# Layer-0 S5 scan: states stored with the blocks innermost and shifted by one chunk, block carries by doubling

## Chip, cores and metric

The kernel runs on one core of a Trainium2 chip. The metric is device time in microseconds (us) of one execution; a smaller number is better. Times of several executions are given as their median with the lowest and highest.

## What is computed

The reference is a stack of four decoder layers over a residual stream `x` of 256 tokens by 1024 channels (batch 1, fp32). Each layer normalises `x`, makes one wide input projection, runs a token mixer (layer 0: S5, 1: GLA, 2: differential attention, 3: Mamba-2 SSD), gates it, adds a cross attention to 256 memory tokens and projects back onto `x`. Only layer 0 matters here. Its mixer, cut to what matters:

```python
# u: 256 tokens x 2048 channels = 128 groups of 16; 64 complex states per group
dr, di = einsum('tgh,gph->tgp', u, bb_re), einsum('tgh,gph->tgp', u, bb_im)
s[t]   = lam_bar * s[t-1] + (dr, di)[t]          # complex, per group and state
y[t]   = einsum('gp,ghp->gh', s_re[t], c_re) - einsum('gp,ghp->gh', s_im[t], c_im) + d_skip * u[t]
g      = gelu(y);  out = g * sigmoid(g @ w_glu) * silu(z)
```

The recurrence is linear, so it can be cut: inside a chunk the response to the chunk's own tokens is a matrix product, and only the state at the chunk's border has to be carried.

## The kernel before, in words

**Tiling of the scan.** A chunk is 4 tokens, so there are 64 chunks. The 128 groups are worked in four units (`ub` 0 to 3) of 32 groups each, by `s5_unit` (line 598). Two groups with their 64 states fill the 128 partitions, so a unit has 16 columns of group pairs (four sub-blocks `sb` of four). A unit's states lie in a tile `E` of 128 partitions x 2 (real, imaginary) x 16 x 64 chunks.

**Steps of one unit.** For each `sb`, VectorE scales the B matrix by powers of lambda (`scaled`, L639 to L644, tiles `q` and `bu`), ScalarE copies it into a padded tile (L656), TensorE transposes it (L661), ScalarE evacuates that (`pm`, L662), TensorE multiplies it with the tokens `V` (L666) and ScalarE copies the chunks' own responses into `E` (L667, one copy of 512 columns). The same scaling gives the C matrix (`cu`, `cp`, L677) and the response inside a chunk (`kt`, L684, and `tm`, eight-buffer `cp`, two-buffer `tm`). Then VectorE runs the recurrence over the 64 chunks of `E`, taken as 8 blocks `J` of 8 chunks `i`:

- L706: seven local steps, each for all 8 blocks at once (`step`, L701 to L704: a product, one addition of the real factor's part, one subtraction, one addition);
- L708: seven carry steps over the blocks, each on the last chunk of one block (L698, L702 to L704 on 16 columns of groups);
- L712: the carry added to the first seven chunks of blocks 1 to 7 (L716 to L719), for the real and the imaginary part.

After a `yield` TensorE makes the output `y` (L730 from `tm` and `V`, L734 from `cp` and `E`, where chunk `j` reads state `j-1`, hence columns 1:64 from 0:63), and ScalarE applies gelu (L736).

In `E` the chunk number is 8J+i with `i` innermost, so one local step reads and writes every eighth float32 of a row, and the factor for a position (tile `lp`, L537) has the groups innermost.

**Order of the tokens.** `x` is loaded with its rows regrouped (L753) so that VectorE's 32x32 transposition (`evac_u`, L779) gives `V` by chunk. Layer 0 keeps this order through its projections; the tokens are put back in order where a result is split into a high and a low half for the output projection (`split`, L114 on ScalarE and L115 on VectorE, called from `xattn` at L428 and `evac_glu` at L847).

**What sets the order of the work.** `layer0` (L745) enlists projections as generators in `self.fill`: four steps of z, the u blocks 2 and 3, then q_mem and z_x (L225). It calls each unit up to its `yield` with raised priority, then gives out some fill (`tick`, 4, 4, 2, 2 steps), then the rest of the unit. A planner lays the instructions out in one fixed order per engine before the run, from those priorities and its own costs; on the chip each engine takes its list in order and waits on semaphores. `V` has two buffers, so the tokens of unit 2 are written after unit 0's output matmuls have read theirs. Powers and factors are made once in `s5_tables` (L500). Weights come by SP's DMA queue into five `raw` buffers.

Of the kernel before, what the change touches and what calls it, by code (L numbers as in the profile page):

```python
# [37 lines left out]
class Net:  # L38
# [139 lines left out]
    def trans_split(self, src, slot, perm=False, gain=None):  # L178

# [3 lines left out]
        for kp in range(2):  # L183
            ps = (self.ps2() if kp else self.ps()).rearrange("p (k t) -> p k t", k=2)
            for kk in range(2):
                for t in range(2):
                    k = kp * 2 + kk
                    nc.tensor.transpose(ps[:, kk, t * P:(t + 1) * P], src[:, t, k * P:(k + 1) * P], self.ident)
            if gain is not None:
                for kk in range(2):  # L190
                    k = kp * 2 + kk
                    self.split(ps[:, kk, :], hi[:, k, :], lo[:, k, :], gain[:, k:k + 1])
            elif perm:
                self.split(ps.rearrange("p k (h s j) -> p (k h) s j", h=2, s=4),
                           *(v[:, kp * 2:kp * 2 + 2, :].rearrange("p k (h j s) -> p (k h) s j", h=2, s=4)
                             for v in (hi, lo)))
            else:
                self.split(ps, hi[:, kp * 2:kp * 2 + 2, :], lo[:, kp * 2:kp * 2 + 2, :])
# [171 lines left out]

    def xattn(self, i, qx, zx, perm=False):
# [35 lines left out]
        for hp in range(2):  # L407
# [92 lines left out]
    def s5_tables(self, p, tp):  # L500
# [36 lines left out]
        lp = p.tile([P, 2, 8, 64], F32, name="s5lp")  # L537
# [52 lines left out]
        for i, (t, n) in enumerate(((pwc, 4), (pwb, 4), (lp[:, :, 0:1, :], 16))):  # L590
# [7 lines left out]
    def s5_unit(self, ub, V, p, tab, fix, gT):  # L598
# [3 lines left out]
        i32, lp, pwc, pwb, lp0 = tab  # L602
# [45 lines left out]
        for sb in range(4):  # L648
# [18 lines left out]
            nc.scalar.copy(E[:, :, ls, :], dps)  # L667
# [54 lines left out]
        for sb in range(4):  # L722
# [5 lines left out]
            for t in range(4):  # L728
# [16 lines left out]
    def layer0(self):  # L745
        nc, tc, a = self.nc, self.tc, self.a
        w = a["s5_w_in"][0]
        with self.pool("l0") as lp_:
            gTs = [lp_.tile([P, 4, 256], F32, tag="brT", name=f"gT{i}", bufs=4) for i in range(4)]
            gT = [gTs[k // 4][:, k % 4, :] for k in range(16)]  # L750
            with self.pool("l0a", "right") as p0:
                xp = [p0.tile([P, DM], F32, name=f"xp{h}") for h in range(2)]
                src = a["x"][0].rearrange("(h j s) d -> h s j d", h=2, s=4)  # L753
                for h in range(2):
                    for s in range(4):
                        (nc.sync if s % 2 else nc.scalar).dma_start(xp[h][32 * s:32 * s + 32, :], src[h, s])
                hT = self.norm_T(xp, self.norm_g[:, 0:8], lambda: self.hT_slot(F32), p0,
                                 True)
                tab = self.s5_tables(lp_, p0)
            with self.pool("s5") as p:  # L760
                bpad = p.tile([P, 2, 16, 32], F32, name="bpad")

                cps = [p.tile([P, 2, 4, 4, 32], F32, name=f"cp{i}") for i in (4, 5, 6, 7)]
                tms = [p.tile([P, 16, P], F32, name="tm1")]
                Es = [p.tile([P, 2, 16, 64], F32, name=f"E{i}") for i in range(2)]
                for _ in range(2):
                    self.t4(p, "V", 2)
                cps = [p.tile([P, 2, 4, 4, 32], F32, name=f"cp{i}") for i in range(4)] + cps
                tms.insert(0, p.tile([P, 16, P], F32, name="tm0"))
                bpps = [p.tile([P, 2, 4, 4, 32], F32, name=f"bpp{i}") for i in range(2)]  # L770
                for t in [bpad] + bpps + tms + cps:
                    nc.gpsimd.memset(t, 0.0)
                Vs, xs = [], []
                zs = [self.hT_slot(F32) for _ in range(2)]

                def evac_u(nb, acc, c):
                    Vs.append(self.t4(p, "V", 2).rearrange("p (h g j) -> p h g j", h=2, j=32))
                    for h in range(2):
                        nc.vector.transpose(Vs[-1][:, h].rearrange("p g j -> p (g j)"), acc[:, h, :])  # L779

                def keep_z(nb, ps):
                    nc.scalar.copy(zs[nb // 2][:, 2 * (nb % 2):2 * (nb % 2) + 2, :], ps)

                us = [self.linear_steps(hT, w, ub * 512, 512, evac_u) for ub in (0, 1)]
                us.append(self.linear2_steps(hT, w, DI, DI // 2, keep_z, lambda: self.acc()[:, 0, :]))
                us += [self.linear_steps(hT, w, ub * 512, 512, evac_u) for ub in (2, 3)]
                us.append(self.qx_zx_steps(xs, hT, w, 2 * DI, False))
                self.fill = us
                self.drain(5)
                self.all_gains()  # L790
                for ub, n in enumerate((4, 4, 2, 2)):
                    unit = self.s5_unit(ub, Vs[ub], p, tab, (bpad, bpps, cps, tms, Es), gT)
                    with tc.high_priority(offset=200):
                        next(unit)
                    self.tick(n)
                    with tc.high_priority(offset=200):
                        next(unit, None)
# [3 lines left out]
            with self.pool("l0b") as p:  # L801
# [36 lines left out]
                def evac_glu(nb, ps):  # L838
# [7 lines left out]
                    pv = lambda t: t.rearrange("p k (h j s) -> p (k h) s j", h=2, s=4)  # L846
                    self.split(br.rearrange("p k (h s j) -> p (k h) s j", h=2, s=4), pv(hi), pv(lo))  # L847
# [701 lines left out]
```

## Time and profile before

| what | value |
|---|---|
| three executions, median (lowest to highest) | 1423.85 us (1422.84 to 1428.41) |
| the profiled execution's own time | 1432.01 us |
| its span in the trace | 1430.3 us |
| busy share of the span, PE / VectorE / ScalarE / GpSimd | 94% / 69% / 57% / 9% |
| mean granted TensorE clock | 0.977 |

The profiled execution took 1432.01 us, of which the span holds all but 1.7 us. PE stands for TensorE's matmuls, PEld for its weight loads, DVE for VectorE, ACT for ScalarE, POOL for GpSimd. Layer 0 takes the first part of the span, and the S5 units lie between about 45 and 262 us. A row of a timeline gives start, length, engine, line, operation, output and inputs, the count of merged instructions, and in brackets the engine's idle time before them with what ended it. A row of groups gives the count, the busy time in us with the mean of one in ns, and after the second bar the idle time before them.

### The profile page before, as it was taken

What the parts mean: (1) busy time and instruction counts of PE and PEld (TensorE: products, weight loads), DVE (VectorE), ACT (ScalarE), POOL (GpSimd) and SP (SyncE); (2) the same over time, 40 slices, a digit from 0 to 9 for tenths busy, and PEclk for the clock granted to TensorE, in tenths of its full rate; (3) what the DMA queues carried; (4) which work ended last, traced back from release to release, by engine and by line L of the source; (5) the groups of instructions that cost most, each with busy time, mean ns of one, the idle gap of its engine ahead of it and who ended that gap; (6) DMA issues with size and microseconds to landing.
All of it is one profiled execution on the core that took longest, in us unless ns stands there. A gap on an engine that the chain in (4) does not pass through costs nothing. (4 is left out here: it accounts for less than half of the span.)

```text
span 1430.3 us, 24119 instructions
## 1 busy us (share of the span) xinstructions
PE 1349.4 (94%) x9482; PEld 1099.7 (77%) x9482; DVE 986.3 (69%) x1802; ACT 809.7 (57%) x1331; POOL 122.3 (9%) x151
## 2 busy tenths in 40 slices
PE   5898887999999999999999999999999998899998
PEld 3575665889998787787787777787777897788976
DVE  6599999686555767664467587767765576666773
ACT  2573550565443568565455566577554467777762
POOL 1310000010002100000102021203002000000000
PEclk9999999999999999999999999999999899999999
DMA  5634122655655545554655445345345463455442
GB/s 166 124 93 134 50 60 82 201 148 161 177 190 179 168 118 167 155 148 133 175 185 169 139 123 172 123 143 156 110 132 153 120 177 103 119 145 143 125 148 74
DMA packets 175667, 199.86 MB, mean 140 GB/s; under 512 B 32330, under 2 KB 112451, under 8 KB 175555
## 3 DMA queue, kind: packets, MB, share of 16 engines
q1 hardware_dynamic: 173442, 193.72, 46.2%
q10 hardware_dynamic: 1280, 3.21, 0.8%
q0 software_dynamic: 832, 1.41, 0.6%
q8 instruction: 74, 1.21, 0.4%
q14 instruction: 39, 0.31, 0.1%
HBM read 194.64 MB, written 1.05 MB: 137 GB/s over the span
## 5 line engine op out<-in xcount | busy, mean ns | idle before, releaser
L115 DVE TENSOR_TENSOR lo<-raw,hi 128x1024 fp32r<-128x1024 f32 x331 | 400.5, 1214 | 242.2 <-ACT hi L114 238.8
L114 ACT CAST hi<-raw 128x1024 fp32r<-128x1024 f32 x331 | 343.6, 1040 | 352.1 <-PE acc L229 221.1
L227 PE MATMUL acc<-hi,hT 128*128 128x512 f32 (+1 forms) x576 | 234.0, 406 | 1.9 <-ACT v L936 1.2
L229 PE MATMUL acc<-hi,hT 128*128 128x512 f32 (+1 forms) x576 | 229.4, 399 | 1.5 <-DVE hT L118 1.3
L228 PE MATMUL acc<-lo,hT 128*128 128x512 f32 (+1 forms) x576 | 228.9, 397 | 0.0
L107 POOL TENSOR_TENSOR rr<-rv,mhalf 128x2 f32<-128x2 f32 (+3 forms) x34 | 71.7, 2108 | 1045.4 <-DVE rv L105 997.9
L227 PEld LDWEIGHTS acc<-hi,hT 128*128 128x128 f32 x576 | 111.3, 193 | 29.1 <-issue 3.4
L229 PEld LDWEIGHTS acc<-hi,hT 128*128 128x128 f32 x576 | 111.1, 193 | 27.6 <-DVE hT L118 2.8
L228 PEld LDWEIGHTS acc<-lo,hT 128*128 128x128 f32 x576 | 111.2, 193 | 22.6 <-issue 0.2
L227 PE MATMUL ps<-hT,hi 128*128 128x256 f32 (+1 forms) x328 | 97.5, 297 | 6.1 <-ACT mt L1405 4.3
L229 PE MATMUL ps<-hT,lo 128*128 128x256 f32 (+1 forms) x328 | 95.5, 291 | 0.6 <-DVE lo L115 0.6
L228 PE MATMUL ps<-hT,hi 128*128 128x256 f32 (+1 forms) x328 | 95.8, 292 | 0.0
L225 PE MATMUL acc<-raw,hT 128*128 128x512 f32 x160 | 79.3, 626 | 0.0
L227 PE MATMUL ps<-ghi,hi 128*128 128x256 f32 x256 | 72.3, 282 | 0.7 <-ACT xt L415 0.7
L229 PE MATMUL ps<-ghi,lo 128*128 128x256 f32 x256 | 71.7, 280 | 0.0
L228 PE MATMUL ps<-glo,hi 128*128 128x256 f32 x256 | 71.5, 279 | 0.0
L227 PEld LDWEIGHTS ps<-hT,hi 128*128 128x128 f32 (+1 forms) x328 | 64.0, 195 | 9.8 <-ACT mt L1405 4.9
L227 PE MATMUL acc<-hT,hi 128*128 128x256 f32 x224 | 65.0, 290 | 1.2 <-ACT xq L462 1.2
L229 PEld LDWEIGHTS ps<-hT,lo 128*128 128x128 f32 (+1 forms) x328 | 63.8, 195 | 1.4 <-DVE lo L115 0.8
L228 PEld LDWEIGHTS ps<-hT,hi 128*128 128x128 f32 (+1 forms) x328 | 64.1, 195 | 0.5
L229 PE MATMUL acc<-hT,lo 128*128 128x256 f32 x224 | 64.1, 286 | 0.0
L228 PE MATMUL acc<-hT,hi 128*128 128x256 f32 x224 | 63.5, 283 | 0.0
(483 smaller groups left out, 2855.6 us busy)
## 6 DMA issues: line engine op xcount, KB each, us to landing
raw<-in_w_out_dram SPq DMA_DIRECT2D x80, 512.0 KB, 3.7
raw<-in_diff_w_in_dram SPq DMA_DIRECT2D x72, 512.0 KB, 3.8
raw<-in_ssd_w_in_dram SPq DMA_DIRECT2D x56, 512.0 KB, 4.4
raw<-in_gla_w_in_dram SPq DMA_DIRECT2D x48, 512.0 KB, 4.0
raw<-in_s_w_in_dram SPq DMA_DIRECT2D x40, 512.0 KB, 4.7
raw<-in_w_mem_kv_dram SPq DMA_DIRECT2D x32, 512.0 KB, 3.7
raw<-in_s_w_glu_dram SPq DMA_DIRECT2D x32, 512.0 KB, 4.0
x<-in_x_dram ACTq DMA_DIRECT2D x1, 1024.0 KB
```

What stands on the lines that cost most here:

```text
L107: nc.gpsimd.tensor_tensor(r, v, self.mhalf[:, :n], ALU.pow)
L114: nc.scalar.copy(hi, src)
L115: nc.vector.tensor_tensor(lo, src, hi.bitcast(F32), SUB)
L225: mm(out, s[0], m[0], start=start, stop=stop)
L227: mm(out, s[0], m[0], start=start, stop=False)
L228: mm(out, s[0], m[1], start=False, stop=False)
L229: mm(out, s[1], m[0], start=False, stop=stop)
```

## The change

`E` is stored with the block number `J` innermost (positions (i J) in place of (J i)), with the chunk's place `i` permuted (`at`: even places first), and shifted by one chunk: a position holds the state in front of its chunk, and position 0 is zero (a GpSimd memset of one column, once per buffer). The copy into `E` becomes three copies (256, 192 and 56 columns a partition). The rows of `x` are loaded in an order that matches. The seven carry steps over blocks become three, by doubling, on 7, 6 and 4 blocks at a time, with three more powers in `lp` and a table `lp7`. The output matmul reads all 64 columns. Putting the tokens back in order writes with a stride of 32 columns, one 256-column row at a time, where it wrote with a stride of 4 columns, two rows at a time. The tables get a pool of their own that is given back before the second half of layer 0.

The diff, cut to its core (in `layer0` the rest is the same code indented once more; `trans_split` only loses an unused branch):

```diff
+    def reorder(self, src, *dst):
+        return [src.rearrange("p (s i j) -> p s i j", s=8, i=4)] + [
+            d.rearrange("p (j i s) -> p s i j", s=8, i=4) for d in dst]
...
             if perm:
-                self.split(mo[:, hs].rearrange("p k (h s j) -> p (k h) s j", h=2, s=4),
-                           *(u[:, hs].rearrange("p k (h j s) -> p (k h) s j", h=2, s=4) for u in (hi, lo)))
+                for k in (2 * hp, 2 * hp + 1):
+                    self.split(*self.reorder(mo[:, k], hi[:, k], lo[:, k]))
...
-        lp = p.tile([P, 2, 8, 64], F32, name="s5lp")
+        lp = p.tile([P, 2, 10, 64], F32, name="s5lp")
...
-        cmul(part(lp, 1), part(lp, 0), part(lp, 0), None)
-        cmul(span(lp, 2, 2), span(lp, 0, 2), rep(part(lp, 1), 2), 2)
-        cmul(span(lp, 4, 4), span(lp, 0, 4), rep(part(lp, 3), 4), 4)
+        cmul(part(lp, 4), part(lp, 0), part(lp, 0), None)
+        every4 = lambda e: tuple(lp[:, c, e:e + 5:4, :] for c in range(2))
+        cmul(every4(1), every4(0), rep(part(lp, 4), 2), 2)
+        for e in (0, 4):
+            cmul(span(lp, e + 2, 2), span(lp, e, 2), rep(part(lp, 5), 2), 2)
+        for e in (7, 8):
+            cmul(part(lp, e + 1), part(lp, e), part(lp, e), None)
...
-        for i, (t, n) in enumerate(((pwc, 4), (pwb, 4), (lp[:, :, 0:1, :], 16))):
+        for i, (t, n) in enumerate(((pwc, 4), (pwb, 4), (lp[:, :, 0:1, :], 16), (lp[:, :, 7:10, :], 16))):
...
-            nc.scalar.copy(E[:, :, ls, :], dps)
+            for d, s, n in ((32, 0, 32), (8, 32, 24), (1, 56, 7)):
+                nc.scalar.copy(E[:, :, ls, d:d + n], dps[:, :, :, s:s + n])
...
-        Ev = E.rearrange("p c g (J i) -> p c g J i", i=8)
+        Ev = E.rearrange("p c g (i J) -> p c g i J", J=8)
+        at = lambda i: i // 2 + 4 * (i % 2)
-        def step(dst, src, e, n):
+        def step(dst, src, f, n):
-            prod = t_([P, 2, 2, 16, n], f"sa{n}")
-            if n == 1:
-                sv, f = src.rearrange("p c g n -> p c (g n)"), bc(lp[:, :, e, gs], 2, 2)
-                vec.tensor_tensor(prod.rearrange("p x c g n -> p x c (g n)"), bc(sv, 1, 2), f, MUL)
-            else:
-                sv, f = src.rearrange("p c g n -> p (c g) n"), lp0[:, :, 0, ub].rearrange("p x c g -> p x (c g)")
-                vec.tensor_tensor(prod.rearrange("p x c g n -> p x (c g) n"), bc(sv, 1, 2), bc(f, 3, n), MUL)
+            prod = t_([P, 2, 2, 16, 8], "sa")[:, :, :, :, :n]
+            sv, f = src.rearrange("p c g n -> p (c g) n"), f.rearrange("p x c g -> p x (c g)")
+            vec.tensor_tensor(prod.rearrange("p x c g n -> p x (c g) n"), bc(sv, 1, 2), bc(f, 3, n), MUL)
...
         for i in range(1, 8):
-            step(Ev[:, :, :, :, i], Ev[:, :, :, :, i - 1], 0, 8)
-        for J in range(1, 8):
-            step(Ev[:, :, :, J:J + 1, 7], Ev[:, :, :, J - 1:J, 7], 7, 1)
-        pv = lambda c: bc(lp[:, c, 0:7, gs].rearrange("p i g -> p g i"), 2, 7)
-        cv = lambda c: bc(Ev[:, c, :, 0:7, 7], 3, 7)
+            step(Ev[:, :, :, at(i), :], Ev[:, :, :, at(i - 1), :], lp0[:, :, 0, ub], 8)
+        for e, n in enumerate((1, 2, 4)):
+            step(Ev[:, :, :, 7, n:], Ev[:, :, :, 7, :8 - n], lp7[:, :, e, ub], 8 - n)
+        pv = lambda c: bc(lp[:, c, 0:7, gs].rearrange("p i g -> p g i"), 3, 7)
+        cv = lambda c: bc(Ev[:, c, :, 7, 0:7], 2, 7)
...
-            dst = Ev[:, c, :, 1:8, 0:7]
+            dst = Ev[:, c, :, 0:7, 1:8]
...
-                        nc.tensor.matmul(y[32 * g:32 * g + 32, t, 1:64], cp[:, c, g, t, :], E[:, c, l0 + g, 0:63],
+                        nc.tensor.matmul(y[32 * g:32 * g + 32, t, :], cp[:, c, g, t, :], E[:, c, l0 + g, :],
...
-                src = a["x"][0].rearrange("(h j s) d -> h s j d", h=2, s=4)
+                    src = a["x"][0].rearrange("(J i h s) d -> h s i J d", J=8, i=4, h=2)
...
-                tab = self.s5_tables(lp_, p0)
+                    tab = self.s5_tables(pt, p0)
...
-                for t in [bpad] + bpps + tms + cps:
+                    for t in [bpad] + bpps + tms + cps + [E[:, :, :, 0:1] for E in Es]:
...
-                    self.split(br.rearrange("p k (h s j) -> p (k h) s j", h=2, s=4), pv(hi), pv(lo))
+                    for k in range(2):
+                        self.split(*self.reorder(br[:, k, :], hi[:, k, :], lo[:, k, :]))
```

## Rows read from the trace of the kernel before

**Rows 1.** The page: busy time of each engine, and VectorE's busy tenths in 40 slices.
```profile
PE 1349.4 (94%) x9482; PEld 1099.7 (77%) x9482; DVE 986.3 (69%) x1802; ACT 809.7 (57%) x1331; POOL 122.3 (9%) x151
...
DVE  6599999686555767664467587767765576666773
```

**Rows 2.** Stretch of the units: length, busy of each engine, granted clock, DMA share.
```profile
48.00:262.00 214.00, 190.62 (x2572) 135.24 (x2573) 189.04 (x419) 98.95 (x231) 18.14 (x17) 0.96 0.32 85
```

**Rows 3.** Waits of PE from 48 to 262 us: total us, times, longest.
```profile
PE ps L734 <- DVE E L719: 12.4, 5, 5.5
PE ps L730 <- ACT gT L736: 4.8, 4, 2.4
...
PE ps L666 <- DVE V L779: 1.2, 2, 0.6
...
PE ps L681 <- ACT kt L685: 0.8, 1, 0.8
```

**Rows 4.** Groups of VectorE's instructions by line and form, 45 to 247 us.
```profile
L701 DVE TENSOR_TENSOR sa<-E,s5tw 128x512 f32<-128x512 f32 x28 | 30.4, 1085 | 0.4
L639 DVE TENSOR_TENSOR q<-ct,s5tw 128x512 f32<-128x512 f32 x32 | 20.9, 686 | 0.2
...
L702 DVE TENSOR_TENSOR E<-E,sa 128x256 f32<-128x256 f32 x28 | 17.5, 626 | 0.4
L716 DVE TENSOR_TENSOR fx<-E,s5lp 128x784 f32<-128x784 f32 x8 | 12.1, 1507 | 0.0
...
L703 DVE TENSOR_TENSOR E<-E,sa 128x128 f32<-128x128 f32 x28 | 11.0, 393 | 0.5
...
L718 DVE TENSOR_TENSOR fx<-fx,fy 128x784 f32<-128x784 f32 x8 | 7.8, 975 | 0.0
L719 DVE TENSOR_TENSOR E<-E,fx 128x784 f32<-128x784 f32 x8 | 7.8, 971 | 0.0
...
L698 DVE TENSOR_TENSOR sa<-E,s5lp 128x64 f32<-128x64 f32 x28 | 7.2, 258 | 0.5
...
L702 DVE TENSOR_TENSOR E<-E,sa 128x32 f32<-128x32 f32 x28 | 5.9, 212 | 0.6
L703 DVE TENSOR_TENSOR E<-E,sa 128x16 f32<-128x16 f32 x28 | 5.4, 191 | 0.6
```

**Rows 5.** VectorE's timeline: table products of 64, 128 and 256 columns, the first unit's start.
```profile
22.62 0.22 DVE L551 TENSOR_TENSOR tab<-s5pw,tab 128x64 f32<-128x64 f32 x1
...
28.11 0.28 DVE L564 TENSOR_TENSOR tab<-s5lp 128x128 f32<-128x128 f32 x1
...
29.66 0.41 DVE L564 TENSOR_TENSOR tab<-s5lp 128x256 f32<-128x256 f32 x1
...
45.52 1.29 DVE L639 TENSOR_TENSOR q<-bt,s5tw 128x512 f32<-128x512 f32 x2 [8.95 <-POOL bt L614]
```

**Rows 6.** Groups of ScalarE's instructions by line and form, 45 to 262 us.
```profile
L667 ACT COPY E<-ps 128x512 f32<-128x512 f32 x16 | 9.4, 586 | 18.1 <-PE ps L666 18.0
...
L685 ACT COPY kt<-ps 128x96 f32<-128x96 f32 x16 | 3.6, 241 | 6.3 <-DVE kt L684 6.2
```

**Rows 7.** One line of VectorE, 262 to 560 us: ns min/median/max, first and last start.
```profile
L115 DVE TENSOR_TENSOR brT<-hT,brT x4: 1093/1110/1114, 330.9 to 375.2; 128x512 fp32r<-128x512 f32 x4
```

**Rows 8.** PE's timeline around its waits for units 0 and 3, and behind the units.
```profile
119.59 7.03 PE L225 MATMUL acc<-raw,hT 128*128 128x512 f32 x16
130.48 0.32 PE L734 MATMUL ps<-E,cp 128*32 128x63 f32 x8 [3.86 <-DVE E L719]
130.72 6.26 PE L225 MATMUL acc<-raw,hT 128*128 128x512 f32 x10
...
232.93 3.72 PE L225 MATMUL acc<-hT,raw 128*128 128x256 f32 x16
242.18 0.44 PE L734 MATMUL ps<-E,cp 128*32 128x63 f32 x8 [5.53 <-DVE E L719]
242.55 6.34 PE L225 MATMUL acc<-hT,raw 128*128 128x256 f32 x16
...
262.00 0.39 PE L227 MATMUL ps<-hhi,hi 128*128 128x256 f32 x1
```

**Rows 9.** VectorE's timeline: unit 0's first local product, first half of its state ready.
```profile
66.40 1.08 DVE L701 TENSOR_TENSOR sa<-E,s5tw 128x512 f32<-128x512 f32 x1
...
129.46 0.96 DVE L719 TENSOR_TENSOR E<-E,fx 128x784 f32<-128x784 f32 x1
```

More of the change, by code (lines that the diff above doesn't have):

```diff
@@ L176, in norm_x, with trans_split @@
                            self.xp)
-    def trans_split(self, src, slot, perm=False, gain=None):
+    def trans_split(self, src, slot, gain=None):
         nc = self.nc
@@ L192, in trans_split @@
                     self.split(ps[:, kk, :], hi[:, k, :], lo[:, k, :], gain[:, k:k + 1])
[L193 to L196, printed above, removed]
             else:
@@ L601, in s5_unit @@
         vec = nc.vector
-        i32, lp, pwc, pwb, lp0 = tab
+        i32, lp, pwc, pwb, lp0, lp7 = tab
         bpad, bpps, cps, tms, Es = fix
@@ L750, in layer0 @@
             gT = [gTs[k // 4][:, k % 4, :] for k in range(16)]
-            with self.pool("l0a", "right") as p0:
-                xp = [p0.tile([P, DM], F32, name=f"xp{h}") for h in range(2)]
-                src = a["x"][0].rearrange("(h j s) d -> h s j d", h=2, s=4)
[L754 to L758, printed above, removed]
-                tab = self.s5_tables(lp_, p0)
@@ L760, in layer0 @@
[L760 to L770, printed above, removed]
-                for t in [bpad] + bpps + tms + cps:
[L772 to L777, printed above, removed]
-                    for h in range(2):
[L779 to L797, printed above, removed]
@@ new lines, in layer0, with evac_u, keep_z @@
+            with self.pool("s5t") as pt:
+                with self.pool("l0a", "right") as p0:
+                    xp = [p0.tile([P, DM], F32, name=f"xp{h}") for h in range(2)]
+                    src = a["x"][0].rearrange("(J i h s) d -> h s i J d", J=8, i=4, h=2)
+                    for h in range(2):
+                        for s in range(4):
+                            (nc.sync if s % 2 else nc.scalar).dma_start(xp[h][32 * s:32 * s + 32, :], src[h, s])
+                    hT = self.norm_T(xp, self.norm_g[:, 0:8], lambda: self.hT_slot(F32), p0,
+                                     True)
+                    tab = self.s5_tables(pt, p0)
+                with self.pool("s5") as p:
+                    bpad = p.tile([P, 2, 16, 32], F32, name="bpad")
+                    cps = [p.tile([P, 2, 4, 4, 32], F32, name=f"cp{i}") for i in (4, 5, 6, 7)]
+                    tms = [p.tile([P, 16, P], F32, name="tm1")]
+                    Es = [p.tile([P, 2, 16, 64], F32, name=f"E{i}") for i in range(2)]
+                    for _ in range(2):
+                        self.t4(p, "V", 2)
+                    cps = [p.tile([P, 2, 4, 4, 32], F32, name=f"cp{i}") for i in range(4)] + cps
+                    tms.insert(0, p.tile([P, 16, P], F32, name="tm0"))
+                    bpps = [p.tile([P, 2, 4, 4, 32], F32, name=f"bpp{i}") for i in range(2)]
+                    for t in [bpad] + bpps + tms + cps + [E[:, :, :, 0:1] for E in Es]:
+                        nc.gpsimd.memset(t, 0.0)
+                    Vs, xs = [], []
+                    zs = [self.hT_slot(F32) for _ in range(2)]
+                    def evac_u(nb, acc, c):
+                        Vs.append(self.t4(p, "V", 2).rearrange("p (h g j) -> p h g j", h=2, j=32))
+                        for h in range(2):
+                            nc.vector.transpose(Vs[-1][:, h].rearrange("p g j -> p (g j)"), acc[:, h, :])
+                    def keep_z(nb, ps):
+                        nc.scalar.copy(zs[nb // 2][:, 2 * (nb % 2):2 * (nb % 2) + 2, :], ps)
+                    us = [self.linear_steps(hT, w, ub * 512, 512, evac_u) for ub in (0, 1)]
+                    us.append(self.linear2_steps(hT, w, DI, DI // 2, keep_z, lambda: self.acc()[:, 0, :]))
+                    us += [self.linear_steps(hT, w, ub * 512, 512, evac_u) for ub in (2, 3)]
+                    us.append(self.qx_zx_steps(xs, hT, w, 2 * DI, False))
+                    self.fill = us
+                    self.drain(5)
+                    self.all_gains()
+                    for ub, n in enumerate((4, 4, 2, 2)):
+                        unit = self.s5_unit(ub, Vs[ub], p, tab, (bpad, bpps, cps, tms, Es), gT)
+                        with tc.high_priority(offset=200):
+                            next(unit)
+                        self.tick(n)
+                        with tc.high_priority(offset=200):
+                            next(unit, None)
```

1 line of the change is left out of this document (removed).

## Prediction

> **What bounds the kernel now.** The page comes first: over the whole span PE is the busy engine, but VectorE's slices show one stretch, from the third to the seventh digit, with 9 in every slice [rows 1]. A slice is 35.8 us, so it lies at about 70 to 250 us, where the S5 units run. The stretch by itself, 48 to 262 us, has PE 190.6 and VectorE 189.0 busy of 214 us, ScalarE 99, DMA 0.32 and a granted clock of 0.96 [rows 2]. Two engines are nearly full and each sometimes waits for the other. Which one ends the waits is read from PE's waits: 12.4 us of them end with the last VectorE instruction of a unit's scan, 4.8 with the gelu (whose ScalarE list stands behind copies that wait for VectorE's `cu`), 1.2 with `V`, 0.8 with `kt`, 19.2 us in all [rows 3]. PE's timeline shows a second cost: behind the wait of 3.86 us, 10 matmuls take 6.26 us where 16 of the same form took 7.03 before it, and behind the wait of 5.53 us, 16 take 6.34 where 16 took 3.72 [rows 8]. That is the lower of the clock's two levels (1.2 in place of 2.4 GHz) for a while. At the earlier pace the 10 would take 4.4, so 1.9 + 2.6 = 4.5 us are lost by this. From VectorE's lateness the stretch therefore loses 19.2 + 4.5 = 23.7 us on PE. Behind 262 us nothing of the change lies on a full engine, so the end of this stretch sets the gain.
>
> **VectorE's scan, part by part.** What strides cost is in the groups [rows 4]. L701 takes 1085 ns for 512 columns reading every eighth float of `E`; L639 takes 686 for 512 columns with a factor repeated along contiguous runs, which is the new form. L716 takes 1507 for 784 with a factor that steps over 64 floats; L718, all contiguous, 975. Contiguous products of 64, 128 and 256 columns take 0.22, 0.28 and 0.41 us [rows 5]. Are runs of 8 in rows of 64 as good as one run? L719 writes `E` in runs of 7 and takes 971, as L718 does. I take the contiguous price; the other bound is the strided one, a gain of nothing on the local steps.
> - Local products, 28 x (1.085 - 0.686) = 11.2 us.
> - L702 on 256 columns, 28 x (0.626 - 0.41) = 6.0.
> - L703 and its twin L704 on 128 columns, 56 x (0.39 - 0.28) = 6.2.
> - L716 and its twin L717, 16 x (1.507 - 0.975) = 8.5. L718 and L719 stay.
> - Carries: 28 steps of 0.258 + 0.212 + two at about 0.19 = 0.85 are 23.7 [rows 4]. The new three steps a unit have products of 448, 384 and 256 columns, sums of 224, 192 and 128, and twice 112, 96 and 64. Read between 0.22 for 64 and 0.686 for 512 these are 1.58 + 1.00 + 1.45 = 4.0 us, 16.1 for four units: 7.6 less.
>
> Together 39.5 us of VectorE's 189.
>
> **What the rest adds.** Tables: two more single products of six instructions, two more of two powers, one of four fewer, and two copies of 384 columns: 12 x 0.22 + 12 x 0.28 - 6 x 0.41 + 2 x 0.4 = 4.3 us by durations, less where neighbours overlap. I cost it at nothing because VectorE then stands 8.95 us waiting for `bt` [rows 5], which is a DMA and a GpSimd copy; without that cover it would be 4.3. The copy into `E`: between 96 columns at 241 ns and 512 at 586 [rows 6] a column costs 0.83 ns, so 256, 192 and 56 take 0.37 + 0.32 + 0.21 = 0.90 in place of 0.59, 5 us for 16. ScalarE is busy 99 of 214 us; what can reach the path is the last copy of a unit and the `pm` evacuations queued behind on ScalarE, which PE's next L666 needs. Between 0 and 5 us; I take 1.0, near the low end because those evacuations stand among fill matmuls on PE. The memset of column 0: GpSimd is busy 18 of 214 us; nothing, and at most a wait of the first copies into `E` behind its other memsets, a few us, taken as zero. The x load has the same eight DMAs of 32 rows of 4 KB in another row order, on the same SP and ScalarE queues and at the same places; no row shows that order. Its cost lies between a slight gain and a few us at the very start; I take zero, since the pieces are equal. The pool for the tables moves no instruction.
>
> **Putting the tokens back.** The split that reorders takes 1110 ns for 512 columns where it writes every fourth float [rows 7], and becomes two of 256 that write every 32nd. L716's stride of 64 floats costs 1507/784 = 1.9 ns a column, L701's of 8 costs 2.1 [rows 4], so a wider stride is no dearer and I expect about 0.65 us each: some 0.2 us more for each of ten pairs, on VectorE and on ScalarE, in a stretch where PE is the full engine. Nothing; without cover it would be 2 us.
>
> **Does the gain arrive?** PE takes its list in order. I walk the list of before with the new durations. Unit 0's state is ready at 129.46 + 0.88 = 130.3 us [rows 9]. In front of that, from the first local product at 66.40 us on [rows 9], VectorE's timeline holds 10 local products, 9 and 17 of the sums, 7 carry steps and two of L716/L717, 10.8 us of the saving, so it would be ready near 119.5; PE gets there at 126.6 [rows 8] and doesn't wait. The same sum for units 2 and 3 gives a margin of about 7 us each time, since PE has then gained some 11 to 17 us itself. So VectorE stops ending PE's waits; PE's own 190 us and its switching between small matmuls become the bound, and the gain is PE's 23.7 us, not VectorE's 39.5. Minus 1.0 for ScalarE: **22.7 us**. The profiled execution (1432.01, span 1430.3) is 0.6% above the median of the runs; the saving is taken off the median as it is: 1423.85 - 22.7 = 1401.
>
> By the rows PE is the limit that remains: while it runs, its matmuls follow one another (16 in 7.03 us [rows 8]). The Trainium skill says otherwise (Perfetto Trace Analysis, "Identifying the Most-Contended Engine"): matmul occupancy is no good measure of how near PE is to its limit, and weight-load busy share is. By that share (135.2 of 214, the row in rows 2) PE would still have a third free, and the sum would be VectorE's whole 39.5 us, 1384. That is the first rival.
>
> **Rivals.**
> 1. *PE has more room than its busy time says.* If the planner packs PE's list better once scans are short, the end follows VectorE: 1423.85 - 39.5 = 1384, and half of the way 1392. For it: PE switches forms often in this stretch. Against it: in rows 8 the matmuls already run without gaps. Chance 0.12.
> 2. *A new order leaves about half of the waits.* The planner lays all lists out anew from fewer and shorter instructions; gelu and `V` waits need not vanish with it. 1423.85 - 12 = 1412. For it: the margin of 7 us is thin. Chance 0.15.
> 3. *The change doesn't do what it says*: runs of 8 cost as strided ones do. Then only the carries and L716/L717 shrink, 16 us on VectorE, of which behind the first unit a few reach PE: about 1419. Against it stands L719. Chance 0.07.
> 4. *Slower: bare scans.* Place: PE's list between `tick` and the output matmuls of units 2 and 3. If the new plan puts the fill (L225) in front, PE waits a whole scan of 7 x 1.6 + 4.0 + 2 x 3.9 = 23 us with nothing to do, and then runs at the low clock for a while. It decides from 23.7 us of bare scan on, just over one scan; two bare scans give 46 - 22.7, about 1447. For it: PE already waits 5.53 us bare before unit 3's output. Against it: unit 3's scan has 32 fill matmuls of z_x around it, and the ticks are not moved. Chance 0.05.
>
> **Numbers.** My case has 0.61, a spread of 6 us either way for the margins and the unknown costs. The range 1388 to 1415 takes in that case, rival 2 and half of rival 1 and leaves 0.06 below and 0.12 above. A measurement of this kernel tells about 0.5%, 7 us, from no change. Faster by more than that: my case, rival 1 and nearly all of rival 2, 0.87; within: rival 3 and the rest, 0.08; slower: rival 4, 0.05.
>
> **What would show it.** Right: L701 near 690 ns, L702 near 410, L703 and L704 near 280, L716 and L717 near 980, and 12 carry steps where there were 28; VectorE's 9s end earlier and have gaps; PE's waits for `E` under 3 us; the first matmul that reads `hhi` at about 240 us, not 262.00 [rows 8]. Wrong: those rows near their old means (rival 3), or the rows as expected with `E` or gelu still ending PE's waits (rivals 2 and 4), or a first `hhi` matmul below 230 (rival 1).

## The result, and the profile after

The changed kernel takes 1409.05 us (median of four executions, 1407.31 to 1414.45) where the kernel before takes 1426.13 on the same chip (1422.84 to 1431.91): ratio 0.9873, 95% interval 0.9843 to 0.9903, a gain of 14 to 22 us. The forecast was 1401, faster, with a range of 1388 to 1415. The profiled execution took 1407.5 us, its span is 1405.4 and the mean granted clock 0.99.

The page of the changed kernel, busy time and VectorE's slices, to be held against [rows 1]:

```profile
PE 1339.2 (95%) x9482; PEld 1090.5 (78%) x9482; DVE 952.7 (68%) x1768; ACT 811.7 (58%) x1373; POOL 124.2 (9%) x153
...
DVE  4789787976557677564567687667766577666773
```

The stretch with 9 in every slice has become one with gaps, as forecast. To compare the stretch of the units ([rows 2]) for equal work, both windows begin 2.2 us ahead of VectorE's first product with `bt` and end at the first matmul that reads `hhi`. The changed kernel's windows (columns as in [rows 2]: length, busy PE, PEld, DVE, ACT, POOL, granted clock, DMA share, GB/s); the second line is a window at the very start, needed below for the x load:

```profile
48.00:243.70 195.70, 188.29 (x2575) 131.22 (x2573) 158.72 (x359) 103.43 (x269) 23.18 (x22) 1.00 0.36 94
...
4.00:8.00 4.00, 0.28 (x1) 0.18 (x1) 0.37 (x2) 0.00 (x0) 0.00 (x0) 1.00 0.26 103
```

The kernel before, the same two places:

```profile
43.30:262.00 218.70, 191.13 (x2574) 135.24 (x2573) 191.45 (x423) 100.97 (x235) 21.26 (x20) 0.95 0.33 86
...
4.00:8.00 4.00, 0.28 (x1) 0.17 (x1) 0.49 (x3) 1.15 (x2) 0.00 (x0) 1.00 0.99 246
```

The stretch is 23.0 us shorter. PE is busy 2.8 us less, with the clock granted in full (1.00 for 0.95), and idle 20.2 us less (7.4 for 27.6). VectorE is busy 32.7 us less (38.3 by the durations of its instructions, added up below, since neighbours overlap). What PE still waits for in the changed kernel, 48 to 243.7 us (total us, times, longest), against [rows 3]:

```profile
PE ps L734 <- ACT gT L740: 2.2, 2, 1.6
PE ps L666 <- issue: 1.7, 1, 1.7
PE ps L222 <- ACT hi L114: 1.0, 1, 1.0
PE ps L671 <- ACT pm L667: 0.7, 2, 0.5
PE ps L738 <- DVE E L723: 0.6, 1, 0.6
PE ps L666 <- ACT bpp L661: 0.5, 2, 0.3
PE ps L734 <- issue: 0.4, 1, 0.4
```

The waits that the prediction laid to VectorE's lateness (for `E`, gelu, `V`, `kt`) fall from 19.2 to 2.8 us: 16.4. Waits that the trace calls "issue", where it shows nothing that PE waited for, fall too, by 4.8. They were not in the forecast's sum; before, from 43 us on, they were these:

```profile
PE ps L661 <- issue: 4.5, 1, 4.5
...
PE ps L730 <- issue: 1.1, 1, 1.1
PE ps L734 <- issue: 0.8, 2, 0.5
...
PE ps L681 <- issue: 0.5, 1, 0.5
```

The longest lies from 43.8 to 48.3 us, in front of the first unit; there the changed kernel's list has fill matmuls (47.60 to 51.30 us). One wait is new, 1.0 us for `hi`. 16.4 + 4.8 - 1.0 is the 20.2.

VectorE's groups in the changed kernel, 30 to 262 us (count, busy us, mean ns, idle before), against [rows 4]:

```profile
L705 DVE TENSOR_TENSOR sa<-E,s5tw 128x512 f32<-128x512 f32 x28 | 19.3, 688 | 0.5
L706 DVE TENSOR_TENSOR E<-E,sa 128x256 f32<-128x256 f32 x28 | 11.8, 421 | 0.4
...
L707 DVE TENSOR_TENSOR E<-E,sa 128x128 f32<-128x128 f32 x28 | 8.4, 298 | 0.5
L708 DVE TENSOR_TENSOR E<-E,sa 128x128 f32<-128x128 f32 x28 | 8.0, 284 | 0.0
...
L720 DVE TENSOR_TENSOR fx<-E,s5lp 128x784 f32<-128x784 f32 x8 | 7.7, 968 | 0.0
...
L705 DVE TENSOR_TENSOR sa<-E,s5tw 128x448 f32<-128x448 f32 x4 | 2.5, 622 | 0.1
L705 DVE TENSOR_TENSOR sa<-E,s5tw 128x384 f32<-128x384 f32 x4 | 2.2, 557 | 0.1
L705 DVE TENSOR_TENSOR sa<-E,s5tw 128x256 f32<-128x256 f32 x4 | 1.7, 422 | 0.1
```

Every price is within 7% of the forecast, the large ones within 3%; L721 is like L720, and the nine sums of the carries, not shown, take 388 to 218 ns. Now where it did not go as forecast. PE's timeline of the changed kernel (start, length, work, in brackets the idle time before it): the first transposition of `x`, unit 3's output ([rows 8] had 5.53 us of waiting and then 16 fill matmuls in 6.34), the first matmul behind the units:

```profile
19.85 3.70 PE L164 MATMUL ps<-ident,xt 128*128 128x128 f32 x16 [12.62 <-DVE xt L154]
...
226.70 0.32 PE L738 MATMUL ps<-E,cp 128*32 128x64 f32 x8 [0.58 <-DVE E L723]
226.95 3.72 PE L220 MATMUL acc<-hT,raw 128*128 128x256 f32 x16
...
243.70 0.39 PE L222 MATMUL ps<-hhi,hi 128*128 128x256 f32 x1 [1.00 <-ACT hi L114]
```

The first transposition in the kernel before:

```profile
15.07 3.69 PE L164 MATMUL ps<-ident,xt 128*128 128x128 f32 x16 [8.77 <-DVE xt L154]
```

From the first transposition to the first `hhi` matmul it is 246.9 us before and 223.9 after, 23.1 less (the forecast was 22.7). But the transposition starts 4.8 us later, and 18.3 of the gain were left at 262.00 [rows 8]. The windows from 4 to 8 us above say how the x load, costed at nothing, comes into this: the eight loads of the same bytes keep 0.26 of the DMA engines busy where they kept 0.99, at 103 GB/s where it was 246. By that share 4 of 16 engines work, at some 26 GB/s each, above the 15.4 of each engine before. The engines that work are not slow; 12 of 16 have nothing to do. Experiments e9 and e10 test this reading.

The load costs the start more than these 4.8 us, because something else there became faster. VectorE's two instructions of L154 end the norm just in front of the transposition. In the kernel before they run beside GpSimd's two loads of `cnat` and the memsets behind these (10.17 to 14.47 us):

```profile
10.23 5.44 DVE L154 TENSOR_SCALAR xt<-xp,rr 128x1024 f32<-128x1024 f32 x2 [0.84 <-DMA tab<-in_s_lam_re_dram]
```

```profile
10.17 0.81 POOL L617 DMA_DIRECT2D cnat<-in_s_c_re_dram  x1
```

In the changed kernel GpSimd starts these loads at 20.38 us, behind L154:

```profile
19.05 1.42 DVE L154 TENSOR_SCALAR xt<-xp,rr 128x1024 f32<-128x1024 f32 x2 [0.84 <-POOL rr L107]
```

That is 4.0 us less. No run moves GpSimd's loads alone, so the cause is argued; but over all runs these two instructions are long (5.44 us) only in the kernel before and in e2, where GpSimd's loads start beside them, and take 1.41 or 1.42 us in the others. What the load costs by itself is read from e1 and e2: 8.3 to 8.5 us at the first transposition.

### The profile page after: what moved, and what is told of

The parts are those of the page before. It is cut to its first block, busy times and chain, and to the rows that moved or that the text cites. A ratio compares the mean times of both kernels' runs of the same rounds, so it can differ in the third digit from the quotient of the medians.

```text
span 1405.4 us, 24122 instructions
## 1 busy us (share of the span) xinstructions
PE 1339.2 (95%) x9482; PEld 1090.5 (78%) x9482; DVE 952.7 (68%) x1768; ACT 811.7 (58%) x1373; POOL 124.2 (9%) x153
## 3 DMA queue, kind: packets, MB, share of 16 engines
q0 software_dynamic: 832, 1.41, 0.5%
## 5 line engine op out<-in xcount | busy, mean ns | idle before, releaser
L222 PEld LDWEIGHTS acc<-hi,hT 128*128 128x128 f32 x576 | 109.9, 191 | 28.9 <-issue 3.4
L224 PEld LDWEIGHTS acc<-hi,hT 128*128 128x128 f32 x576 | 109.6, 190 | 27.4 <-DVE hT L118 2.7
L220 PE MATMUL acc<-raw,hT 128*128 128x512 f32 x160 | 76.4, 609 | 0.0
L222 PEld LDWEIGHTS ps<-hT,hi 128*128 128x128 f32 (+1 forms) x328 | 64.1, 195 | 10.2 <-ACT mt L1410 5.2
```

Of the source, the lines that this page charges most:

```text
L220: mm(out, s[0], m[0], start=start, stop=stop)
L222: mm(out, s[0], m[0], start=start, stop=False)
L224: mm(out, s[1], m[0], start=False, stop=stop)
```

## Experiments

The theory: PE bounds the stretch once VectorE is off its path; the gain there is the strides', and the new order of the rows in the x load costs about 5 us. Rivals: VectorE still ends the stretch; the doubling made the gain; the reorder or the copies into `E` ate the missing part. No run puts the old strides back alone, so their share is what is left when the other parts have been taken away one by one. In the table, median and ratio are from the timed executions, the two starts (us) from the profiled one. Ratios are to the kernel before, timed beside each group of runs. The groups ran on different chips, with medians of the kernel before between 1426.46 and 1428.14 us, so runs of different groups are compared by ratio.

| run | median us | ratio, 95% | first transposition | first `hhi` matmul |
|---|---|---|---|---|
| a0_after | 1410.64 | 0.9899, 0.9878 to 0.9919 | 19.77 | 243.68 |
| e1_oldrows | 1405.14 | 0.9859, 0.9837 to 0.9881 | 11.32 | 237.48 |
| e2_before_newrows | 1434.88 | 1.0045, 1.0028 to 1.0062 | 23.35 | 266.83 |
| e4_seqcarry | 1410.77 | 0.9891, 0.9871 to 0.9911 | 19.95 | 241.32 |
| e6_halfstate | 1408.94 | 0.9845, 0.9814 to 0.9877 | 19.48 | 237.07 |
| e7_onecopy | 1412.39 | 0.9883, 0.9865 to 0.9901 | 19.66 | 243.31 |
| e8_plainsplit | 1413.06 | 0.9886, 0.9869 to 0.9903 | 20.00 | 245.48 |
| e9_pairs | 1423.44 | 0.9976, 0.9961 to 0.9991 | 29.42 | 252.50 |
| e10_singles | 1414.35 | 0.9913, 0.9890 to 0.9937 | 19.25 | 245.35 |
| e5_permuted | 1404.09 | 0.9852, 0.9828 to 0.9875 | 10.90 | 235.94 |
| e12_permuted_again | 1405.30 | 0.9841, 0.9821 to 0.9862 | 11.19 | 236.45 |
| e11_pooldma | 1405.41 | 0.9843, 0.9824 to 0.9863 | 11.19 | 236.32 |

From the `hhi` matmul to the end the profiled executions of the table need 1164 to 1170 us, so a difference at `hhi` below some 6 us can't be followed to the end in one execution; there the medians decide.

**a0_after**: the changed kernel itself, once more beside the others. No edit.

> The changed kernel itself, as the base for the runs beside it. Theory 1 (the load of x in the new row order keeps only about a quarter of the DMA engines busy, and all of layer 0 starts later by that): the first transposition on PE again near 19.9 us, where it was 15.1 before the change, and the first matmul that reads hhi near 243.7. Theory 2 (the late start was a chance of that one execution): the first transposition near 15 us and the first hhi matmul near 239.

The time and both places came out as in the first runs.

**e1_oldrows**: the changed kernel with the row order of the x load of before.

```diff
-                    src = a["x"][0].rearrange("(J i h s) d -> h s i J d", J=8, i=4, h=2)
+                    src = a["x"][0].rearrange("(h j s) d -> h s j d", h=2, s=4)
```

> The changed kernel with the row order of the x load from before, so that layer 0 sees its tokens in another order than the scan takes them for; the instructions are otherwise the same. Theory 1 (the row order costs the late start): DMA share from 4 to 8 us near 1.0 in place of 0.26, first transposition on PE near 15 us, 4 to 5 us off the time of the changed kernel in the same job. Theory 2 (chance): the same time as the changed kernel within 2 us. If a later start only meets a wait that is there anyway (the bt copy that VectorE waits for), the first transposition is early and the time falls by less than 2 us.

Measured: 5.5 us below a0_after. Its windows and PE's timeline:

```profile
4.00:8.00 4.00, 0.28 (x1) 0.18 (x1) 0.37 (x2) 1.15 (x2) 0.00 (x0) 1.00 1.03 259
```

```profile
11.32 3.69 PE L164 MATMUL ps<-ident,xt 128*128 128x128 f32 x16 [4.81 <-DVE xt L154]
...
237.48 0.39 PE L222 MATMUL ps<-hhi,hi 128*128 128x256 f32 x1 [1.49 <-ACT hi L114]
```

With rows of one stride all engines work again. The first transposition comes at 11.32 us, not near the expected 15, since L154 is short here (1.42 us) where it is long in the kernel before. PE starts 8.5 us earlier and has 6.2 of them left at `hhi`. Some of the rest is lost at VectorE's first B product, which waits for `bt` in both kernels, but less far apart (VectorE's timeline of e1, then of the changed kernel: 43.70 against 50.21, 6.5 us):

```profile
43.70 1.29 DVE L644 TENSOR_TENSOR q<-bt,s5tw 128x512 f32<-128x512 f32 x2 [7.19 <-POOL bt L619]
```

```profile
50.21 1.29 DVE L644 TENSOR_TENSOR q<-bt,s5tw 128x512 f32<-128x512 f32 x2 [6.27 <-POOL bt L619]
```

**e2_before_newrows**: the reverse, the kernel before with the new row order.

```diff
-                src = a["x"][0].rearrange("(h j s) d -> h s j d", h=2, s=4)
+                src = a["x"][0].rearrange("(J i h s) d -> h s i J d", J=8, i=4, h=2)
```

> The kernel before with the new row order of the x load alone (layer 0 then sees its tokens in another order than the scan takes them for). Theory 1 (the row order costs the late start by itself): first transposition on PE near 19.9 us and 4 to 5 us slower than before. Theory 2 (chance, or a matter of the whole change): the same time as before within 2 us.

Measured: 0.45% slower, 4 to 9 us (6.7 by the medians). The first transposition comes at 23.35 us, 8.3 later than before and not near the expected 19.9, since L154 is long here as in the kernel before. The first `hhi` matmul comes 4.8 us later (266.83 for 262.00). So the load order costs much the same in either kernel, with all else equal: 8.3 and 8.5 us at the start, 4.8 and 6.2 at `hhi`, 6.7 and 5.5 of time. Its price is 5 to 7 us, and it is the part missing from the forecast.

**e4_seqcarry**: the new layout, but seven carry steps one after the other in place of three by doubling.

```diff
-        for e, n in enumerate((1, 2, 4)):
-            step(Ev[:, :, :, 7, n:], Ev[:, :, :, 7, :8 - n], lp7[:, :, e, ub], 8 - n)
+        for J in range(1, 8):
+            step(Ev[:, :, :, 7, J:J + 1], Ev[:, :, :, 7, J - 1:J], lp7[:, :, 0, ub], 1)
```

> The changed kernel with the seven carry steps over the blocks one after the other again, in the new layout. VectorE gets about 7.6 us more work, some 1.9 us a unit. Theory 1 (PE is the bound of the stretch now and VectorE has slack in front of each of PE's reads of E): 0 to 2 us slower than the changed kernel, PE's waits for E under 3 us. Rival (VectorE still sets the end): 6 to 8 us slower, with PE's waits for E up by as much.

VectorE's groups of the carries in this run:

```profile
L705 DVE TENSOR_TENSOR sa<-E,s5tw 128x64 f32<-128x64 f32 x28 | 7.7, 274 | 0.7
L706 DVE TENSOR_TENSOR E<-E,sa 128x32 f32<-128x32 f32 x28 | 6.1, 218 | 0.6
L707 DVE TENSOR_TENSOR E<-E,sa 128x16 f32<-128x16 f32 x28 | 5.4, 194 | 0.7
L708 DVE TENSOR_TENSOR E<-E,sa 128x16 f32<-128x16 f32 x28 | 5.1, 183 | 0.0
```

They take 24.3 us where the doubled ones take 16.4, so VectorE works 7.9 us more. The kernel takes 1410.77 us where a0_after takes 1410.64, and PE's waits for `E` in this run grow only to:

```profile
PE ps L738 <- DVE E L723: 2.0, 2, 1.5
```

That is 1.4 us more than in the changed kernel, and another 0.4 is for `V`: VectorE had room for most of these 7.9 us. The doubling buys nothing that can be measured here; the change has its whole gain without it. But the time stayed the same for a second reason too. The planner laid PE's list out anew, and in the new order the same 2574 matmuls keep PE busy 6.3 us less. The changed kernel, e4 and, for below, e6, each from 48 us to its last matmuls before `hhi`:

```profile
48.00:243.00 195.00, 188.29 (x2574) 131.22 (x2572) 158.02 (x357) 102.73 (x268) 23.18 (x22) 1.00 0.36 93
```

```profile
48.00:241.00 193.00, 182.02 (x2574) 128.33 (x2574) 162.69 (x421) 102.86 (x268) 23.14 (x22) 1.00 0.37 97
```

```profile
48.00:237.00 189.00, 175.64 (x2062) 124.07 (x2060) 156.70 (x355) 104.31 (x270) 23.15 (x22) 0.97 0.39 101
```

Much of the difference is one place. In the changed kernel's list, 22 of L634's small matmuls alternate two by two with output matmuls from 167.56 to 172.7 us, while a row of 32 takes 1.15 us:

```profile
106.33 1.15 PE L634 MATMUL ps<-ident,cnat 128*64 128x64 f32 x32
...
167.56 0.33 PE L634 MATMUL ps<-ident,cnat 128*64 128x64 f32 x2
167.82 0.30 PE L734 MATMUL ps<-V,tm 128*32 128x64 f32 x2
```

In e4 these too stand in one row of 32. So e4's `hhi` comes 2.4 us earlier although PE is idle 4.3 us longer, and with PE's list held fixed the doubling may be worth up to these 4.3 us.

**e6_halfstate**: output matmuls of the imaginary part alone.

```diff
-                for c in range(2):
+                for c in (1,):
```

> The changed kernel without the output matmuls of the states' real part (256 on fp32 columns, 512 records in the trace, of the 1024 of that line); the output lacks that part. Theory 1 (PE is the bound of the stretch): the first hhi matmul comes earlier by about PE's time for them, 16 sub-blocks of 4 times 8 records at some 14 ns each, 7 us. Rival (VectorE's scan or the chain through E still sets the end): under 2 us earlier, with longer waits of PE for E.

PE's waits in this run, 48 to 237 us:

```profile
PE ps L738 <- DVE E L723: 4.0, 1, 4.0
PE ps L734 <- ACT gT L740: 3.1, 6, 0.7
PE ps L222 <- ACT hi L114: 3.1, 1, 3.1
```

With 512 matmuls fewer, `hhi` comes 6.6 us earlier than in a0_after, near the 7 expected. Not all of it is the price of these matmuls, for this list has no alternation either: PE is busy 12.7 us less than in the changed kernel but 6.4 less than in e4 (rows above), and `hhi` comes 4.3 us earlier than in e4. Either way somewhat more than half of what is taken from PE comes off the stretch: PE's busy time is the main bound, but not alone. The waits for `E`, gelu and `hi` now come to 10.2 us, where the changed kernel has 3.8: VectorE and ScalarE are close behind PE, and much more taken from PE would not come off. This rests on the trace alone. The median (1408.94) has too wide a spread (1402.52 to 1410.70) to show 6.6 us, and behind `hhi` this execution needs 1170.3 us where a0_after's needs 1164.6.

**e7_onecopy**: one copy into `E` in place of three, without the places permuted.

```diff
-            for d, s, n in ((32, 0, 32), (8, 32, 24), (1, 56, 7)):
-                nc.scalar.copy(E[:, :, ls, d:d + n], dps[:, :, :, s:s + n])
+            nc.scalar.copy(E[:, :, ls, 1:], dps[:, :, :, :63])
```

> The changed kernel with one copy into E in place of three (the responses go to the neighbouring column, not to the place of the next chunk, so the states are those of another order). ScalarE has about 5 us less work. My term for it on the path was 1.0 us: the time falls by 0 to 2 us. Rival (the pm evacuations behind the copies hold PE up): 3 to 5 us.

`hhi` comes 0.4 us earlier, and the ratio is that of a0_after within the intervals. The three copies take 14.8 us for 16 sets (372, 325 and 223 ns, 0.92 a set) where one took 9.4 [rows 6], as forecast, and next to nothing of it reaches PE.

**e8_plainsplit**: the splits behind the output projection without putting the tokens in order.

```diff
-                for k in (2 * hp, 2 * hp + 1):
-                    self.split(*self.reorder(mo[:, k], hi[:, k], lo[:, k]))
+                self.split(mo[:, hs], hi[:, hs], lo[:, hs])
...
-                    for k in range(2):
-                        self.split(*self.reorder(br[:, k, :], hi[:, k, :], lo[:, k, :]))
+                    self.split(br, hi, lo)
```

> The changed kernel without the reordering of tokens in front of the output projection of layer 0 (plain splits; the tokens stay in the scan's order). VectorE and ScalarE each lose 20 strided instructions of about 0.65 us and get 10 plain ones of about 0.65. Theory 1 (hidden behind PE): within 1 us of the changed kernel. Rival (the strided writes hold the last projections up): 2 us or more.

No gain: the ratio is that of a0_after within the intervals, and it takes 232.1 us from `hhi` to the run of 12 norm transpositions of layer 1 (245.48 to 477.57), where the changed kernel needs 231.0 (243.70 to 474.72). The reorder is hidden, as forecast.

**e9_pairs** and **e10_singles** ask why the load is slow: each 32-row load cut into two of 2 x 8 rows, or into four of 8 rows with one stride.

```diff
+                            for i in (0, 2):
+                                (nc.sync if s % 2 else nc.scalar).dma_start(
+                                    xp[h][32 * s + 8 * i:32 * s + 8 * i + 16, :], src[h, s, i:i + 2])
```

> The changed kernel with each of its eight loads of x issued as two, of 2 by 8 rows in place of 4 by 8 (the same rows to the same places). Theory 1 (a transfer is dealt to as many DMA engines as its outermost extent, here 4): only 2 engines work, DMA share near 0.13 from 4 to 8 us, the first transposition on PE 6 to 10 us later than 19.8. Rival (the distance of 128 KB between neighbouring rows is slow to read): DMA share and start as in the changed kernel, within 2 us.

```diff
+                            for i in range(4):
+                                (nc.sync if s % 2 else nc.scalar).dma_start(
+                                    xp[h][32 * s + 8 * i:32 * s + 8 * i + 8, :], src[h, s, i])
```

> The changed kernel with each of its eight loads of x issued as four of 8 rows (one stride of 128 KB, the same rows to the same places). Theory 1 (the outermost extent, now 8, sets how many engines work): DMA share of 0.5 or more while x is loaded, the load bounded by 16 issues a queue of some 0.42 us, 6.7 us, first transposition between 13 and 17 us, 2 to 5 us faster than the changed kernel. Rival (the distance of the rows is slow): a rate near 104 GB/s as in the changed kernel, first transposition at 19 us or later.

e9's window and first transposition:

```profile
4.00:8.00 4.00, 0.28 (x1) 0.18 (x1) 0.37 (x2) 0.00 (x0) 0.03 (x1) 1.00 0.13 50
```

```profile
29.42 3.70 PE L164 MATMUL ps<-ident,xt 128*128 128x128 f32 x16 [22.57 <-DVE xt L154]
```

e10's window from 2 to 4 us, before its pace was set by something else:

```profile
2.00:4.00 2.00, 0.00 (x0) 0.00 (x0) 0.51 (x3) 0.91 (x2) 0.49 (x3) 1.00 0.51 117
```

An outermost extent of 4 keeps 0.26 of the engines busy, one of 2 keeps 0.13, one of 8 (for a moment) 0.51, one of 32 all: by these shares 4, 2, 8 and 16 of 16. That both queues together reach no more than that says that their loads go to the same few engines; the trace has no share of each engine by itself. The rival, that the distance of 128 KB between neighbouring rows is slow to read, is out: e9 and e10 keep that distance, and the share follows the extent. The Trainium skill has this rule (DMA: Bandwidth & Descriptors, section "Why a DMA increments its semaphore by 16 and not by 1"): a transfer runs on the largest number of engines up to 16 that divides the slowest dimension (of more than one step) of both its patterns, source and destination, and on the queues of SP and ScalarE these are the lowest-numbered ones. The four shares agree with it. e9 pays 9.6 us more than the changed kernel at the first transposition and some 11 us of time (ratio 0.9976 for 0.9899). e10 does not win back what it should by the share of 0.51: behind 4 us the share falls to 0.28, because each queue's 16 issues, 0.27 us long, come some 0.79 us apart (from 0.8 to 12.7 us on SP). What holds the issues back was not tried. e10 therefore tells nothing on time, only the share does.

**e5_permuted**: one-stride loads and the new layout together. The rows go in with a single stride of 32 rows, and the order within a block of 32 is made by TensorE: the 32 transpositions of layer 0 become matmuls with a permuted unit matrix, made by one GpSimd copy.

```diff
+        rows = self.ident
+        if whole:
+            rows = pool.tile([P, P], F32, name="rowperm")
+            self.nc.gpsimd.tensor_copy(rows.rearrange("p (s i J) -> p s i J", s=4, i=4),
+                                       self.ident.rearrange("p (s J i) -> p s i J", s=4, i=4))
...
+                        if whole:
+                            nc.tensor.matmul(ps[:, kk, t * P:(t + 1) * P], xn[t][:, k * P:(k + 1) * P], rows,
+                                             start=True, stop=True)
...
-                    src = a["x"][0].rearrange("(J i h s) d -> h s i J d", J=8, i=4, h=2)
+                    src = a["x"][0].rearrange("(q h s) d -> h s q d", h=2, s=4)
```

> The changed kernel with rows of x loaded in steps of 8 rows (one stride for 32 rows), and the order of the tokens made by TensorE: the transpositions of layer 0 multiply with a permuted unit matrix. Theory 1: DMA share near 1.0 from 4 to 8 us, first transposition near 15 us, about 4.8 us faster than the changed kernel. Rival (the DMA engines are kept from work by the distance of the rows in memory and not by how the transfer is cut): DMA share stays between 0.26 and 1, and less than 2.5 us is gained.

PE's timeline of this run:

```profile
10.90 5.32 PE L170 MATMUL ps<-rowperm,xt 128*128 128x128 f32 x32 [4.79 <-DVE xt L159]
...
235.94 0.38 PE L231 MATMUL ps<-hhi,hi 128*128 128x256 f32 x1 [0.75 <-ACT hi L114]
```

1404.09 us, 6.5 below a0_after; the share in the window from 4 to 8 us is 1.02. **e12_permuted_again** is the same kernel in another group of runs:

> The version with x rows in steps of 8 and a permuted unit matrix once more, on another chip or at another time. If the load of x is what the change gives back, the ratio to the kernel before is again about 0.985, 5 to 7 us below the changed kernel's 0.987 to 0.990; if the first reading was chance, about 0.989.

1405.30 us, ratio 0.9841. This kernel beats the one before, and the changed kernel as a0_after in both groups, and it keeps the whole of the forecast gain: 22.4 and 21.9 us by the medians beside it (1426.46 and 1427.22).

**e11_pooldma**: e5 with two late loads issued by GpSimd. In the changed kernel ScalarE issues the residual `x` and the memory tokens at 240.01 to 242.2 us, right in front of the `hi` split for which PE waits 1.0 us.

```diff
-            nc.scalar.dma_start(m[t], a["mem"][0, t * P:(t + 1) * P, :])
+            nc.gpsimd.dma_start(m[t], a["mem"][0, t * P:(t + 1) * P, :])
...
-        nc.scalar.dma_start(self.x, a["x"][0].rearrange("(t p) d -> p t d", p=P))
+        nc.gpsimd.dma_start(self.x, a["x"][0].rearrange("(t p) d -> p t d", p=P))
```

> That version with the three late loads (x for the residual, and the two of mem) issued by GpSimd, which is idle then, in place of ScalarE, where their issues of 0.4 to 1.1 us stand between the last gelu and the first split of weights (L114), for which PE waits 0.7 to 1.0 us. Theory: first hhi matmul 1 to 2 us earlier, time 0 to 2 us lower. Rival (the split waits for something else, such as the buffer of hi): no change at the first hhi matmul.

No gain (1405.41; `hhi` at 236.32). The wait for `hi` is gone, and PE waits 2.0 us for VectorE's `lo` a moment later.

## Why the prediction was right, and what it missed

- **VectorE's scan** (39.5 us): right. With the means above: local products 28 x (1085 - 688) = 11.1 for 11.2; the 256-column sums 5.7 for 6.0; the 128-column ones 5.6 for 6.2; L716/L717 8.6 for 8.5; carries 16.4 us where 16.1 was forecast, 7.3 saved for 7.6. Runs of 8 floats cost as one run does, as the prediction took from L719. Rival 3 is out.
- **PE becomes the bound; its 23.7, not VectorE's 39.5**: right in the main. e6 shows it from PE's side (`hhi` 4.3 to 6.6 us earlier with 512 matmuls less), e4 from VectorE's (7.9 us more work, 1.8 us more of waits for it). Rival 1, that PE has a third free, did not come: the weight-load share is 131.2 of 195.7 now, and PE is busy 188.3. But PE's busy time is no floor: e4's order needs 6.3 us less of it for the same matmuls, so that a little of rival 1's condition, a better packed list, is there. A third free, as the prediction read it out of the weight-load share (the Trainium skill, Perfetto Trace Analysis, "Identifying the Most-Contended Engine"), no run shows.
- **The sum within the stretch**, 19.2 + 4.5 - 1.0 = 22.7, measured 23.0 to 23.1: the total is right, its terms less so, and that they come out so near the total is luck. The 19.2 gave 16.4, since 2.8 us of such waits stayed, nearly all gelu. The 4.5 for the lower clock shows as 2.8 of busy time, in which the new order of PE's matmuls also has its part. What makes up for it is 4.8 us of issue waits, most of it the one at 43.8 us, mostly ahead of the window of [rows 3] and in no term. The 1.0 for ScalarE's copies is about zero (e7), and the 1.0 us of new waiting is for `hi`, behind the units.
- **The margin of 7 us**: too large. Unit 0's state was forecast for 119.5 us (the prediction adds 0.88 us for L719 where [rows 9] has 0.96, which moves this by 0.1), 122.6 with VectorE's later start (69.54 for 66.40); it is ready at 123.9 (122.98 + 0.96), and PE reads it at 125.58: 1.6 us. Unit 3's is 0.6 us late. It was enough for rivals 2 and 4 not to come: waits for `E` are 0.6 us in all.
- **Tables, memset, reorder, copies, at nothing**: right. VectorE still waits 6.27 us for `bt`; the two splits take 0.65 us each as estimated; e7 and e8 win nothing by undoing them.
- **The x load, at zero "since the pieces are equal"**: wrong, and the one term that moved the time. The prediction's own upper bound, a few us at the very start, was the better value: 8.3 to 8.5 us at the first transposition, of which the changed kernel shows 4.8 since L154 became 4.0 us shorter, a term that the prediction doesn't have; and 5 to 7 us of time by e1, e2 and e5. The pieces were equal in bytes and number; what differed was the nest of rows, 4 of 8 in place of one run of 32.
- **The time**: 1401 was counted down from 1423.85, the median of three; beside the result the kernel before took 1426.13, so 2.3 of the 8 us between 1401 and 1409.05 are the base. From the new base the gain is 17.1 us for 22.7, 5.6 less, which is the price of the load.

## What to carry to other kernels

Where two engines are both nearly full, cost the saving on the one by the waits of the other: past that point, shorter work on it (here the doubling) buys little or nothing, and the next gain has to come off the engine that is left. On PE that can be the order alone: two kinds of small matmuls alternating two by two took several times as long as the same in rows. Put the innermost loop of a VectorE recurrence over contiguous floats; runs of 7 or 8 were already as good as one long run. A load that regroups rows should keep one long outermost run with one stride (32 kept all DMA engines busy, 8, 4 and 2 did not), and an order within that is cheaper made by a permuted unit matrix in a transposition that happens anyway.

## What was unexpected of the hardware

- The same 1 MB of rows of 4 KB in the same eight issues runs at 246 or at 103 GB/s by the nest of its pattern alone, with 16 or 4 engines. By these shares each engine is faster when 4 work (26 GB/s) than when 16 do (15.4), so the rate falls to a 2.4th and not to a quarter.
- An issue of such a nested load also takes longer on its queue: 0.63 to 1.28 us each in the changed kernel, 0.38 to 0.44 in e1. In e10, where each issue lasts 0.27 us, the issues nevertheless came 0.79 us apart.
- VectorE's L154, 0.75 us an instruction elsewhere, took 4.79 us once where GpSimd's loads and memsets started beside it (the kernel before). In e1 and e10, where another VectorE instruction (L510) met them, that one took 3.77 and 3.67 us for 0.21.
- The same 2574 matmuls of the stretch keep PE busy 188.3 or 182.0 us by their order alone, at a granted clock of 1.00 both times.
- PE's clock: in the kernel before it was granted 0.93 from 48 to 88 us, 0.91 from 120 to 160 and 0.84 from 240 to 262, behind waits; in the changed kernel it is 1.00 in every part of the stretch, and in e6, whose waits for `E` are longer, 0.97 (0.82 from 208 to 237 us).
